# A pinned order for VectorE and ScalarE, a fourth load place and fewer warming products in the down stage of a decoder layer

## The chip, the cores and the metric

The kernel runs on one core of a Trainium2 chip. The metric is the device time of one execution in microseconds (us), as the median of several runs. TensorE (PE; its weight loads PEld) multiplies, VectorE (DVE), ScalarE (ACT) and GpSimd (POOL) work on tiles, and SyncE (SP) issues most transfers.

## The reference

One layer of a hybrid decoder, in float32, with 256 tokens and a model width of 2048:

```
h = RMSNorm(x);  z = h @ W_in
y = concat(PoolMixer(z_pool), MLA(z_q, z_kv, z_kr), MemXAttn(z_mq, mem)) @ W_o
x = x + y
h = RMSNorm(x)
x = x + (silu(conv(h @ W_gate)) * (h @ W_up)) @ W_down
```

The feed-forward width is 5632, and `conv` is causal over three tokens. The change lies in the last product, `a @ W_down`, where `a` is 256 x 5632 and `W_down` is 5632 x 2048, and in the first microseconds of the kernel.

## The kernel before, in words

**Splitting.** Every float32 weight is cut into a high part and a remainder. `split_w` (L88) does this for up to 1024 columns: ScalarE casts the weight to `wh` (L94), and VectorE subtracts `wh` from the weight to give `wl` (L95). Each of the two has three places. TensorE then makes three products of 512 columns for each sum: high by high, remainder of the activation by high, and high by remainder. In the down stage these are L740, L741 and L742, the three lines of `prod`. L742 alone reads `wl`.

**Loads.** `load_w` (L82) brings 1 MB of weights, 2048 columns, to one of three places of the tag `wr`. SP issues these loads in order (L85), and each waits until the place it needs is free.

**Stages.** First the memory's keys and values, before whose first product 16 products of ones keep TensorE at work (L159, L160) while the first loads arrive; then the input projection, the attention heads and the output projection; then `gemm_t` (L108, L111) for gate and up, 44 times, with `glu` after each; and from about 791 us the down stage.

**The down stage** (L735 to L823) makes two passes `c`, one for each half of the output's columns. A pass goes over 22 pairs `j` of feature blocks. A pair's weights are four blocks of 128 x 512, and its result is 2 token tiles by 2 column tiles.

- `plain` (L744) makes the 8 sums in the usual way, from two splits of 1024 columns. Thirteen pairs of a pass go this way: `j` = 0, 1, 3, 5, ..., 19, 20, 21. The last goes bank by bank.
- `seven` (L755) makes them from 7 sums of combined blocks, for `j` = 2, 4, ..., 18. VectorE forms the weights' differences: L760 two blocks at once (1024 columns), L763 and L764 one each. Splits follow: b11 (512 columns), b2, t13 and t24 (1024 each). t13 and t24 read the differences, which lie in `dn`; the trace calls their remainders `wl<-dn` and the others `wl<-wr`. Three of the seven sums go to the result's own banks, four to common ones (`com`).
- `common` (L775) fetches x1 for the output through POOL's queue (step 0), adds up the common sums (step 1), and adds these, scaled, to x1 (step 2).
- `finish` (L795) adds the own sums and writes the output. For the first pass it is called behind the first `plain` of the second.

`dn` is one tile of 16 blocks of 512 columns: blocks 0 to 7 hold the differences of two `seven`s in turn, 8 to 11 the common sums, 12 to 15 the output. It takes the place of the activation `h2`, which the gate and up products read.

**What sets the order.** The kernel is written in a framework that builds each engine's queue from its own estimate of when operands are ready. A queue is therefore not in the order of the source unless something forces it. Semaphores are set from the data that each instruction reads and writes. On the chip each queue runs in the order so built.

Of the kernel before, what the change touches and what calls it, by code (L numbers as in the profile page):

```python
# [11 lines left out]
F32 = mybir.dt.float32  # L12
# [3 lines left out]
ALU = mybir.AluOpType  # L16
AX = mybir.AxisListType

P = 128
# [17 lines left out]
STG = 2048  # L37
HS = 1024
NN = 512

PAIRS = KF // 2
SEVEN = tuple(range(2, 20, 2))
# [18 lines left out]
def layer(ctx, tc, xT_d, xn_d, memT_d, vec_d, tab_d, w_z_d, w_mqkr_d, w_q_d, w_kv_d, w_mem_d, w_pool_d, w_o_d,  # L61
          w_g_d, w_u_d, w_dn_d, out_d):
    nc = tc.nc

    const = ctx.enter_context(tc.tile_pool(name="const", bufs=1))
    stage = ctx.enter_context(tc.tile_pool(name="stage", bufs=1))
# [5 lines left out]
    def nm(s):  # L72
        uid[0] += 1
        return f"{s}_{uid[0]}"
# [7 lines left out]
    def load_w(src, n, cut=STG):  # L82
        raw = stage.tile([P, STG], F32, tag="wr", name=nm("wr"), bufs=3)
        for c in range(0, n, cut):
            nc.sync.dma_start(raw[:, c:min(n, c + cut)], src[:, c:min(n, c + cut)])  # L85
        return raw

    def split_w(raw, o, n, cut=HS):  # L88

        hi = stage.tile([P, HS], F32R, tag="wh", name=nm("wh"), bufs=3)  # L90
        lo = stage.tile([P, HS], F32R, tag="wl", name=nm("wl"), bufs=3)
        for c in range(0, n, cut):
            e = min(n, c + cut)
            nc.scalar.copy(hi[:, c:e], raw[:, o + c:o + e])  # L94
            nc.vector.tensor_tensor(lo[:, c:e], raw[:, o + c:o + e], hi[:, c:e].bitcast(F32), op=ALU.subtract)  # L95
        return hi, lo

    def gemm_t(ps, raw, o, act, ks, first=True, last=True):
# [57 lines left out]
    warm = const.tile([P, 1], F32, name="warm")  # L156
    nc.scalar.copy(warm[:], eps[:])
    ps = ps_aux()
    for _ in range(16):  # L159
        nc.tensor.matmul(ps[:, 0:P], ones[:], ones[:], start=True, stop=True)  # L160

    def rsqrt_(dst, src, scale):
# [73 lines left out]
    raw0 = stage.tile([P, STG], F32, tag="wr", name=nm("wr"), bufs=3)  # L236
# [181 lines left out]
    for m in range(6):  # L418
        raw = load_w(w_z_d[m], STG)
# [18 lines left out]
    for i in range(2):  # L438
        o = slice(2 * i, 2 * i + 2)
# [293 lines left out]


    dn = big.tile([P, 16, NN], F32, tag="act", name="dn")  # L735
    cnt = [0]

    def prod(ps, a, b, first, last):

# [4 lines left out]
    def plain(c, j, own, first, last, by_bank=False):  # L744
        raw = load_w(w_dn_d[c, j], STG)
        ws = [split_w(raw, k * HS, HS) for k in range(2)]
        order = [(k, t, n) for k in range(2) for t in range(NT) for n in range(2)]
        if by_bank:
            order.sort(key=lambda o: o[1:])
        for k, t, n in order:  # L750
            a = [aT[j][:, k, o + t * P:o + (t + 1) * P] for o in (0, T)]
            s = n if k == 0 else 1 - n
            prod(own[t, n], a, [w[:, s * NN:(s + 1) * NN] for w in ws[k]], first and k == 0, last and k == 1)

    def seven(c, j, own, com, first, last):  # L755
        raw = load_w(w_dn_d[c, j], STG)
        r3 = raw[:].rearrange("p (b n) -> p b n", n=NN)
# [7 lines left out]
        Ff = F.rearrange("p b n -> p (b n)")  # L765
        t13 = split_w(Ff, 0, HS)
        t24 = split_w(Ff, HS, HS)
        for (b, s), f, ps, own_ in (((b11, 0), 6, com[0], False), ((b2, 0), 5, own[0, 1], True),
                                    ((b2, 1), 0, own[0, 0], True), ((t13, 0), 2, com[1], False),
                                    ((t13, 1), 4, com[3], False), ((t24, 0), 3, com[2], False),  # L770
                                    ((t24, 1), 1, own[1, 0], True)):
            prod(ps, [aT[j][:, i, f, :] for i in range(2)], [w[:, s * NN:(s + 1) * NN] for w in b],
                 first and not own_, last and not own_)

    def common(c, com, step):  # L775

        v1, u2, u3, u5 = (dn[:, 8 + i, :] for i in range(4))
        if step == 0:
            for t in range(NT):
                for n in range(2):  # L780
                    o = c * HS + n * NN
                    nc.gpsimd.dma_start(dn[:, 12 + 2 * t + n, :], x1s[:, t, o:o + NN])
        elif step == 1:
            nc.scalar.copy(v1, com[0])
            nc.vector.tensor_tensor(u2, v1, com[2], op=ALU.add)
            nc.vector.tensor_tensor(u3, u2, com[3], op=ALU.add)
            nc.vector.tensor_tensor(u5, u3, com[1], op=ALU.add)
            nc.vector.tensor_tensor(u2, u2, com[1], op=ALU.add)
        else:
            for i, u in enumerate((v1, u2, u3, u5)):  # L790
                t = i // 2
                nc.vector.scalar_tensor_tensor(dn[:, 12 + i, :], u, rc[:, t:t + 1], dn[:, 12 + i, :],
                                               op0=ALU.mult, op1=ALU.add)

    def finish(c, own, eng):  # L795
        for t in range(NT):
            for n in range(2):
                o = dn[:, 12 + 2 * t + n, :]
                nc.vector.scalar_tensor_tensor(o, own[t, n], rc[:, t:t + 1], o, op0=ALU.mult, op1=ALU.add)
                eng.dma_start(out_d[t][:, c * HS + n * NN:c * HS + (n + 1) * NN], o)  # L800

    done = None
    for c in range(2):
        own_ps, com_ps = (ps_main, ps_aux) if c else (ps_aux, ps_main)
        own = {(t, n): own_ps()[:] for t in range(NT) for n in range(2)}
        com = None
        for j in range(PAIRS):
            if j in SEVEN:
                if com is None:
                    com = [com_ps()[:] for _ in range(4)]  # L810
                seven(c, j, own, com, j == SEVEN[0], j == SEVEN[-1])
# [12 lines left out]

# [83 lines left out]
```

## Time and profile before

| | before |
|---|---|
| median of 3 runs | 1030.2 us (1030.11 to 1031.09) |
| the profiled execution, its time | 1030.77 us |
| its span, first to last instruction | 1028.7 us |
| PE busy | 1018.4 us, 99% of the span |
| DVE busy | 760.3 us, 74% |
| ACT busy | 572.6 us, 56% |
| POOL busy | 15.3 us, 1% |
| transfers | 198.06 MB, mean 193 GB/s |
| TensorE's granted clock | 9 or more tenths in all 40 slices |

The span is what the trace covers; the execution's own time also holds what lies around it. A busy time counts an engine's work, not its waits. PE's ends are modelled and its products overlap, so an interval between two starts says more than the duration of one. In rows of a timeline a bracket holds the engine's idle time before the instruction and what ended it.

### The profile page before, as it was taken

The page shows a single profiled execution, that of the slowest core. Times are in us where ns is not written, and L with a number is a line of the kernel's source. Part 1 is how long each engine was busy: PE and PEld are TensorE (multiplying, and loading weights), DVE is VectorE, ACT ScalarE, POOL GpSimd, SP SyncE. Part 2 cuts the span into 40 slices and gives each one's busy share as a digit, 9 for nine tenths or more (in the row PEclk, how much of TensorE's full clock was granted, in tenths as well). Part 3 has the DMA queues.
Part 4 walks back from the last instruction along what each step waited for, and adds up shares of the span by engine and source line. Part 5 has one row for each costly group of instructions (what it writes and reads, how often), then busy time and mean ns, then how long its engine had stood idle before and what let it go on. Part 6 is the DMA issues. An engine that isn't in the chain of part 4 may idle for free.

```text
span 1028.7 us, 14089 instructions
## 1 busy us (share of the span) xinstructions
PE 1018.4 (99%) x5366; PEld 868.1 (84%) x5366; DVE 760.3 (74%) x1140; ACT 572.6 (56%) x850; POOL 15.3 (1%) x33
## 2 busy tenths in 40 slices
PE   9999999999999999999999999999999999989998
PEld 7798888877888888888888888888888888877886
DVE  7967689756577776776767677676767788877886
ACT  7847576644566455555555555554555465544653
POOL 0000000000000000000000000000000000010000
PEclk9999999999999999999999999999999999999999
DMA  9575444333765555545545555555555555565552
GB/s 343 204 264 202 147 181 164 133 124 123 232 213 181 194 195 177 202 176 193 196 175 203 180 189 197 175 202 183 186 200 207 201 210 204 205 245 205 205 198 89
DMA packets 30611, 198.06 MB, mean 193 GB/s; under 512 B 3536, under 2 KB 4048, under 8 KB 8656
## 3 DMA queue, kind: packets, MB, share of 16 engines
q1 hardware_dynamic: 28368, 189.44, 52.0%
q0 software_dynamic: 1888, 7.34, 1.9%
q8 instruction: 42, 0.69, 0.3%
q10 hardware_dynamic: 288, 0.38, 0.1%
q14 instruction: 25, 0.20, 0.1%
HBM read 192.96 MB, written 4.19 MB: 192 GB/s over the span
## 4 chain that ended last, share of the span: by engine, by line
PE 95%; DMA 2%; DVE 2%; ACT 0%; issue 0%; SPq 0%; DVEq 0%
PE psm L108 35%; PE psm L111 18%; PE psm L127 6%; PE psm L125 6%; PE psm L126 6%; PE psm L742 3%; PE psa L742 3%; PE psm L740 3%; PE psm L741 3%; PE psa L741 3%; PE psa L740 3%; DMA wr<-in_w_dn 1%; DVE wl L95 1%; PE psa L223 1%; PE psa L392 1%; DMA wr<-in_w_mem 1%
## 5 line engine op out<-in xcount | busy, mean ns | idle before, releaser
L94 ACT CAST wh<-wr 128x1024 fp32r<-128x1024 f32 (+2 forms) x360 | 362.0, 1007 | 366.7 <-PE psm L108 177.5
L95 DVE TENSOR_TENSOR wl<-wr,wh 128x1024 fp32r<-128x1024 f32 (+2 forms) x360 | 417.8, 1169 | 193.9 <-ACT wh L94 191.5
L108 PE MATMUL psm<-h,wh 128*128 128x512 f32 x1408 | 353.1, 392 | 0.0
L108 PEld LDWEIGHTS psm<-h,wh 128*128 128x128 f32 x1408 | 253.2, 189 | 45.2
L111 PEld LDWEIGHTS psm<-h,wl 128*128 128x128 f32 x1408 | 192.1, 190 | 13.7
L111 PE MATMUL psm<-h,wl 128*128 128x256 f32 x1408 | 196.3, 282 | 0.0
L94 ACT CAST wh<-dn 128x1024 fp32r<-128x1024 f32 x36 | 36.2, 1053 | 30.1 <-PE psm L741 15.1
L95 DVE TENSOR_TENSOR wl<-dn,wh 128x1024 fp32r<-128x1024 f32 x36 | 42.4, 1219 | 9.0 <-ACT wh L94 9.0
L685 DVE SCALAR_TENSOR_TENSOR gc<-g,vec,gc 128x255 f32<-128x255 f32 x88 | 42.2, 480 | 1.5
L108 PE MATMUL psm<-xg,wh 128*128 128x512 f32 x160 | 43.0, 401 | 0.0
L742 PE MATMUL psm<-wl,aT 128*128 128x512 f32 x104 | 40.6, 391 | 0.0
L742 PE MATMUL psa<-wl,aT 128*128 128x512 f32 x104 | 40.6, 390 | 0.0
L740 PE MATMUL psm<-wh,aT 128*128 128x512 f32 x104 | 40.5, 390 | 0.0
L740 PE MATMUL psa<-wh,aT 128*128 128x512 f32 x104 | 40.5, 389 | 0.0
L741 PE MATMUL psm<-wh,aT 128*128 128x512 f32 x104 | 40.5, 389 | 0.0
L741 PE MATMUL psa<-wh,aT 128*128 128x512 f32 x104 | 40.5, 389 | 0.0
L125 PE MATMUL psm<-wh,cat 128*128 128x512 f32 x96 | 38.5, 401 | 0.0
L127 PE MATMUL psm<-wl,cat 128*128 128x512 f32 x96 | 37.8, 394 | 0.0
L126 PE MATMUL psm<-wh,cat 128*128 128x512 f32 x96 | 37.6, 392 | 0.0
L108 PEld LDWEIGHTS psm<-xg,wh 128*128 128x128 f32 x160 | 28.8, 189 | 4.9
L760 DVE TENSOR_TENSOR dn<-wr 128x1024 f32<-128x1024 f32 x18 | 22.0, 1223 | 12.9 <-DMA wr<-in_w_dn 12.4
L742 PE MATMUL psa<-wl,aS 128*128 128x512 f32 x63 | 24.4, 395 | 3.6 <-DVE wl L95 3.6
(227 smaller groups left out, 1365.3 us busy)
## 6 DMA issues: line engine op xcount, KB each, us to landing
wr<-in_w_g SPq DMA_DIRECT2D x44, 1024.0 KB, 4.8
wr<-in_w_u SPq DMA_DIRECT2D x44, 1024.0 KB, 4.8
wr<-in_w_dn SPq DMA_DIRECT2D x44, 1024.0 KB, 4.8
wr<-in_w_o SPq DMA_DIRECT2D x16, 1024.0 KB, 4.9
wr<-in_w_z SPq DMA_DIRECT2D x10, 1024.0 KB, 4.8
wr<-in_w_mqkr SPq DMA_DIRECT2D x8, 576.0 KB, 3.7
wr<-in_w_mem SPq DMA_DIRECT2D x4, 1024.0 KB, 7.0
wr<-in_w_mem SPq DMA_DIRECT2D x7, 512.0 KB, 9.0
```

The lines of the kernel that those rows point to most:

```text
L94: nc.scalar.copy(hi[:, c:e], raw[:, o + c:o + e])
L95: nc.vector.tensor_tensor(lo[:, c:e], raw[:, o + c:o + e], hi[:, c:e].bitcast(F32), op=ALU.subtract)
L108: nc.tensor.matmul(ps[:, :2 * T], hi[:, i * P:(i + 1) * P], act(k), start=first and c + i == 0, stop=False, skip_group_check=True)
L111: nc.tensor.matmul(ps[:, T:2 * T], lo[:, i * P:(i + 1) * P], act(k)[:, 0:T], start=False, stop=end and i == len(kc) - 1, skip_group_check= ...
L125: nc.tensor.matmul(ps, xh, hi[:, i, o], start=first and i == 0, stop=False)
L126: nc.tensor.matmul(ps, xl, hi[:, i, o], start=False, stop=False)
L127: nc.tensor.matmul(ps, xh, lo[:, i, o], start=False, stop=last and i == nk - 1)
L685: nc.vector.scalar_tensor_tensor(gc[:, d:T], g[:, 0:T - d], v(w, f), gc[:, d:T], op0=ALU.mult, op1=ALU.add)
L740: nc.tensor.matmul(ps, a[0], b[0], start=first, stop=False)
L741: nc.tensor.matmul(ps, a[1], b[0], start=False, stop=False)
L742: nc.tensor.matmul(ps, a[0], b[1], start=False, stop=last)
L760: nc.vector.tensor_tensor(F[:, 0:2], r3[:, 1:3], r3[:, 0:2], op=ALU.subtract)
```

## The change

A helper `keep` puts an instruction behind whatever the source wrote last for the same engine. It is used on all splits and differences of the down stage from `j` = 3 of the first pass on, and on the sums of `common` and `finish`. Steps 1 and 2 of `common` and the first pass's `finish` move between the two splits of a `plain` call (`between`): step 1 into `j` = 20, step 2 into `j` = 21, `finish` into `j` = 0 of the second pass. In `seven` the order is now L760's differences, b11, the two single differences, b2, t13, t24, and the differences have four blocks of `dn` instead of eight, whose halves swap roles from call to call. The four blocks that this frees, 4 to 7, are the place of every fourth load of the down stage. The warming products at the start are 13 instead of 16.

```diff
+    def keep(ins, on=True):
+        return tc.keep_in_program_order(ins) if on else ins
...
-            nc.scalar.copy(hi[:, c:e], raw[:, o + c:o + e])
-            nc.vector.tensor_tensor(lo[:, c:e], raw[:, o + c:o + e], hi[:, c:e].bitcast(F32), op=ALU.subtract)
+            keep(nc.scalar.copy(hi[:, c:e], raw[:, o + c:o + e]), kept)
+            keep(nc.vector.tensor_tensor(lo[:, c:e], raw[:, o + c:o + e], hi[:, c:e].bitcast(F32), op=ALU.subtract),
+                 kept)
...
-    for _ in range(16):
+    for _ in range(13):
         nc.tensor.matmul(ps[:, 0:P], ones[:], ones[:], start=True, stop=True)
...
+    def load_dn(c, j):
+        cnt[1] += 1
+        if cnt[1] % 4:
+            return load_w(w_dn_d[c, j], STG)
+        raw = dn[:, 4:8].rearrange("p b n -> p (b n)")
+        nc.sync.dma_start(raw, w_dn_d[c, j])
+        return raw
...
-        ws = [split_w(raw, k * HS, HS) for k in range(2)]
+        ws = [split_w(raw, 0, HS, kept=kept)]
+        if between is not None:
+            between()
+        ws.append(split_w(raw, HS, HS, kept=kept))
...
-        F = dn[:, 4 * (cnt[0] % 2):4 * (cnt[0] % 2) + 4, :]
-        nc.vector.tensor_tensor(F[:, 0:2], r3[:, 1:3], r3[:, 0:2], op=ALU.subtract)
-        b11 = split_w(raw, 0, NN)
-        b2 = split_w(raw, 2 * NN, HS)
-        nc.vector.tensor_tensor(F[:, 2], r3[:, 2], F[:, 0], op=ALU.subtract)
-        nc.vector.tensor_tensor(F[:, 3], r3[:, 3], F[:, 2], op=ALU.subtract)
-        t13 = split_w(Ff, 0, HS)
-        t24 = split_w(Ff, HS, HS)
+        i = cnt[0] % 2
+        F13, F24 = dn[:, 2 * i:2 * i + 2], dn[:, 2 - 2 * i:4 - 2 * i]
+        keep(nc.vector.tensor_tensor(F13, r3[:, 1:3], r3[:, 0:2], op=ALU.subtract), kept)
+        b11 = split_w(raw, 0, NN, kept=kept)
+        keep(nc.vector.tensor_tensor(F24[:, 0], r3[:, 2], F13[:, 0], op=ALU.subtract), kept)
+        keep(nc.vector.tensor_tensor(F24[:, 1], r3[:, 3], F24[:, 0], op=ALU.subtract), kept)
+        b2 = split_w(raw, 2 * NN, HS, kept=kept)
+        t13 = split_w(F13.rearrange("p b n -> p (b n)"), 0, HS, kept=kept)
+        t24 = split_w(F24.rearrange("p b n -> p (b n)"), 0, HS, kept=kept)
...
+            kept = c > 0 or j > SEVEN[0]
...
-                plain(c, j, own, j == 0, j == PAIRS - 1, by_bank=j == PAIRS - 1)
-            if j == 0 and done is not None:
-                finish(0, done, nc.gpsimd)
+                between = None
+                if j == 0 and done is not None:
+                    between = lambda o=done: finish(0, o, nc.gpsimd)
+                elif j >= PAIRS - 2:
+                    between = lambda s=j - PAIRS + 3: common(c, com, s)
+                plain(c, j, own, j == 0, j == PAIRS - 1, kept, between, j == PAIRS - 1)
...
-            if j == PAIRS - 3:
-                common(c, com, 1)
-            if j == PAIRS - 2:
-                common(c, com, 2)
```

## Rows read from the trace of the kernel before

**Rows 1.** All instructions of L742: duration ns min/median/max, first and last start us.

```profile
L742 PE MATMUL psa<-wl,aT x104: 389/389/497, 791.8 to 905.9; 128*128 128x512 f32 x104
L742 PE MATMUL psm<-wl,aT x104: 388/389/504, 906.6 to 1024.3; 128*128 128x512 f32 x104
```

**Rows 2.** Timeline of PE (start us, us, what), 28 undisturbed products, first and last.

```profile
899.81 0.39 PE L742 MATMUL psa<-wl,aT 128*128 128x512 f32 x1
...
905.93 0.39 PE L742 MATMUL psa<-wl,aT 128*128 128x512 f32 x1
```

**Rows 3.** PE's waits, 790 to 1029 us: total us, times, longest.

```profile
PE psa L742 <- DVE wl L95: 3.6, 2, 2.8
PE psm L742 <- DVE wl L95: 0.4, 1, 0.4
```

**Rows 4.** Timeline of PE at late products.

```profile
836.31 0.45 PE L742 MATMUL psm<-wl,aS 128*128 128x512 f32 x1
...
919.53 0.39 PE L740 MATMUL psa<-wh,aS 128*128 128x512 f32 x1
922.67 0.50 PE L742 MATMUL psa<-wl,aS 128*128 128x512 f32 x1 [2.76 <-DVE wl L95]
923.01 0.39 PE L741 MATMUL psa<-wh,aS 128*128 128x512 f32 x1
...
934.52 0.73 PE L742 MATMUL psa<-wl,aS 128*128 128x512 f32 x2 [0.86 <-DVE wl L95]
```

**Rows 5.** Timeline of DVE at the longest wait.

```profile
919.53 1.23 DVE L760 TENSOR_TENSOR dn<-wr 128x1024 f32<-128x1024 f32 x1 [2.94 <-DMA wr<-in_w_dn]
...
921.40 2.35 DVE L95 TENSOR_TENSOR wl<-dn,wh 128x1024 fp32r<-128x1024 f32 x2
```

**Rows 6.** Timeline of DVE, PEld and PE at one of six undisturbed calls.

```profile
855.16 2.36 DVE L95 TENSOR_TENSOR wl<-dn,wh 128x1024 fp32r<-128x1024 f32 x2 [1.50 <-ACT wh L94]
...
856.44 0.19 PEld L742 LDWEIGHTS psm<-wl,aS 128*128 128x128 f32 x1
...
856.60 0.39 PE L742 MATMUL psm<-wl,aS 128*128 128x512 f32 x1
```

**Rows 7.** Timeline of DVE, the first operations of one `seven`.

```profile
947.36 1.22 DVE L760 TENSOR_TENSOR dn<-wr 128x1024 f32<-128x1024 f32 x1
948.50 0.68 DVE L95 TENSOR_TENSOR wl<-wr,wh 128x512 fp32r<-128x512 f32 x1
949.10 0.68 DVE L763 TENSOR_TENSOR dn<-wr,dn 128x512 f32<-128x512 f32 x1
949.82 0.69 DVE L764 TENSOR_TENSOR dn<-wr,dn 128x512 f32<-128x512 f32 x1
950.42 1.22 DVE L95 TENSOR_TENSOR wl<-wr,wh 128x1024 fp32r<-128x1024 f32 x1
```

**Rows 8.** Timeline of DVE, the third sum of `finish` at the end of the first pass.

```profile
904.99 0.75 DVE L799 SCALAR_TENSOR_TENSOR dn<-psa,rc,dn 128x512 f32<-128x512 f32 x1 [0.61 <-PE psa L742]
```

**Rows 9.** The page's DMA issues (KB, median us to landing), and one load in the chain.

```profile
wr<-in_w_dn SPq DMA_DIRECT2D x44, 1024.0 KB, 4.8
...
911.57 7.94 DMA wr<-in_w_dn
```

**Rows 10.** Timeline of SP, the fourth load of the down stage and the one behind.

```profile
790.18 6.55 SPq L85 DMA_DIRECT2D wr<-in_w_dn  x2
```

**Rows 11.** L160 by stretches: us, PE busy (x) PEld busy (x), PEclk, DMA share, GB/s.

```profile
3.00:5.00 2.00, 2.00 (x11) 2.00 (x11) 1.00 0.87 277
...
6.76:7.50 0.74, 0.74 (x7) 0.74 (x6) 1.00 0.90 280
```

**Rows 12.** Timeline of PE and ACT at the start.

```profile
7.51 0.48 PE L125 MATMUL psm<-wh,mg 128*128 128x512 f32 x1
...
8.87 1.15 ACT L94 CAST wh<-wr 128x512 fp32r<-128x512 f32 x2 [1.65 <-DMA wr<-in_w_mem]
...
11.27 0.51 PE L126 MATMUL psm<-wh,mg 128*128 128x512 f32 x1 [0.29 <-DVE mg L136]
```

More of the change, by code (lines that the diff above doesn't have):

```diff
@@ L85, in load_w, with split_w @@
             nc.sync.dma_start(raw[:, c:min(n, c + cut)], src[:, c:min(n, c + cut)])
-        return raw
-    def split_w(raw, o, n, cut=HS):
+        return raw[:]
+    def keep(ins, on=True):
+        return tc.keep_in_program_order(ins) if on else ins
+    def split_w(raw, o, n, cut=HS, kept=False):
         hi = stage.tile([P, HS], F32R, tag="wh", name=nm("wh"), bufs=3)
@@ L235, in layer @@
     xg = mp.tile([P, KD, 2 * T], F32R, tag="cat", name="xg")
-    raw0 = stage.tile([P, STG], F32, tag="wr", name=nm("wr"), bufs=3)
+    raw0 = stage.tile([P, STG], F32, tag="wr", name=nm("wr"), bufs=3)[:]
     for a, b in ((0, 1), (1, 2), (2, 4)):
@@ L735, in layer @@
     dn = big.tile([P, 16, NN], F32, tag="act", name="dn")
-    cnt = [0]
+    cnt = [0, 0]
+    def load_dn(c, j):
[5 more added lines that the diff above has]
+        return raw
     def prod(ps, a, b, first, last):
@@ L742, in prod, with plain @@
         nc.tensor.matmul(ps, a[0], b[1], start=False, stop=last)
-    def plain(c, j, own, first, last, by_bank=False):
-        raw = load_w(w_dn_d[c, j], STG)
-        ws = [split_w(raw, k * HS, HS) for k in range(2)]
+    def plain(c, j, own, first, last, kept, between=None, by_bank=False):
+        raw = load_dn(c, j)
+        ws = [split_w(raw, 0, HS, kept=kept)]
+        if between is not None:
+            between()
+        ws.append(split_w(raw, HS, HS, kept=kept))
         order = [(k, t, n) for k in range(2) for t in range(NT) for n in range(2)]
@@ L753, in plain, with seven @@
             prod(own[t, n], a, [w[:, s * NN:(s + 1) * NN] for w in ws[k]], first and k == 0, last and k == 1)
-    def seven(c, j, own, com, first, last):
-        raw = load_w(w_dn_d[c, j], STG)
-        r3 = raw[:].rearrange("p (b n) -> p b n", n=NN)
-        F = dn[:, 4 * (cnt[0] % 2):4 * (cnt[0] % 2) + 4, :]
+    def seven(c, j, own, com, first, last, kept):
+        raw = load_dn(c, j)
+        r3 = raw.rearrange("p (b n) -> p b n", n=NN)
+        i = cnt[0] % 2
         cnt[0] += 1
-        nc.vector.tensor_tensor(F[:, 0:2], r3[:, 1:3], r3[:, 0:2], op=ALU.subtract)
-        b11 = split_w(raw, 0, NN)
-        b2 = split_w(raw, 2 * NN, HS)
-        nc.vector.tensor_tensor(F[:, 2], r3[:, 2], F[:, 0], op=ALU.subtract)
-        nc.vector.tensor_tensor(F[:, 3], r3[:, 3], F[:, 2], op=ALU.subtract)
-        Ff = F.rearrange("p b n -> p (b n)")
-        t13 = split_w(Ff, 0, HS)
-        t24 = split_w(Ff, HS, HS)
+        F13, F24 = dn[:, 2 * i:2 * i + 2], dn[:, 2 - 2 * i:4 - 2 * i]
[6 more added lines that the diff above has]
+        t24 = split_w(F24.rearrange("p b n -> p (b n)"), 0, HS, kept=kept)
         for (b, s), f, ps, own_ in (((b11, 0), 6, com[0], False), ((b2, 0), 5, own[0, 1], True),
@@ L783, in common @@
         elif step == 1:
[L784 to L788, printed above, removed]
+            keep(nc.scalar.copy(v1, com[0]))
+            for u, a, b in ((u2, v1, com[2]), (u3, u2, com[3]), (u5, u3, com[1]), (u2, u2, com[1])):
+                keep(nc.vector.tensor_tensor(u, a, b, op=ALU.add))
         else:
@@ L791, in common @@
                 t = i // 2
-                nc.vector.scalar_tensor_tensor(dn[:, 12 + i, :], u, rc[:, t:t + 1], dn[:, 12 + i, :],
-                                               op0=ALU.mult, op1=ALU.add)
+                keep(nc.vector.scalar_tensor_tensor(dn[:, 12 + i, :], u, rc[:, t:t + 1], dn[:, 12 + i, :],
+                                                    op0=ALU.mult, op1=ALU.add))
     def finish(c, own, eng):
@@ L798, in finish @@
                 o = dn[:, 12 + 2 * t + n, :]
-                nc.vector.scalar_tensor_tensor(o, own[t, n], rc[:, t:t + 1], o, op0=ALU.mult, op1=ALU.add)
+                keep(nc.vector.scalar_tensor_tensor(o, own[t, n], rc[:, t:t + 1], o, op0=ALU.mult, op1=ALU.add))
                 eng.dma_start(out_d[t][:, c * HS + n * NN:c * HS + (n + 1) * NN], o)
@@ L810, in layer @@
                     com = [com_ps()[:] for _ in range(4)]
-                seven(c, j, own, com, j == SEVEN[0], j == SEVEN[-1])
+                seven(c, j, own, com, j == SEVEN[0], j == SEVEN[-1], kept)
             else:
-                plain(c, j, own, j == 0, j == PAIRS - 1, by_bank=j == PAIRS - 1)
-            if j == 0 and done is not None:
-                finish(0, done, nc.gpsimd)
+                between = None
[4 more added lines that the diff above has]
+                plain(c, j, own, j == 0, j == PAIRS - 1, kept, between, j == PAIRS - 1)
             if j == PAIRS - 6:
                 common(c, None, 0)
-            if j == PAIRS - 3:
-                common(c, com, 1)
-            if j == PAIRS - 2:
-                common(c, com, 2)
         done = own
```

## The prediction

> **What bounds the kernel now.** I read four views, from the whole to the single product. The page comes first: TensorE is its busiest engine by far, so only time in which TensorE waits can be won. Next come all instructions of L742, the third line of `prod`. The down stage has 26 `plain` calls of 8 sums and 18 `seven` calls of 7, three products each: 1002 products. L742 first starts at 791.8 us and last at 1024.3 us [rows 1], so 999 steps took 232.5 us. An undisturbed step takes (905.93 - 899.81) / 27 = 0.2267 us [rows 2], and 999 of them 226.5 us. The stage thus holds 6.0 us that are not products following each other. That is all that a change of order can win there.
>
> Then I read who ended TensorE's waits in this stage: always VectorE's L95, the remainder `wl` of a split, 4.0 us in three waits [rows 3]. The product rows say what a wait costs. From 919.53 to 922.67 is 3.14 us, and the step after it, to 923.01, takes 0.34: together 3.03 more than two plain steps, of which 2.76 are shown as idle. So a wait costs its idle time, 0.16 beside it, and 0.11 in the step behind. By that rule the wait at 934.52 (0.86 idle) costs 1.13, and the third one (0.4 idle) 0.66. Sum: 4.8 us. Beyond these there are six places where a product is late by 0.04 to 0.17 us, about 0.5 us together; the one at 836.31 stands for them (0.45 us long where 0.39 is usual) [rows 4].
>
> Last I read VectorE around the longest wait. At 919.53 it begins L760, the differences of the **next** `seven`, after 2.94 us in which it only waited for that load to land. Behind it, at 921.40, come the two remainders of the **current** `seven`'s differences, for which TensorE stands [rows 5]. So the order on VectorE is the cause: an instruction that TensorE needs late stands ahead of one that it needs now, and the former waits for a load.
>
> **The change, part by part.**
>
> *The pinned order.* From `j` = 3 of the first pass on, VectorE and ScalarE follow the written order, in which a `seven`'s splits t13 and t24 and both splits of the following `plain` stand ahead of the next L760. What this does can be seen in the run before, for at six of the 18 `seven`s the queue happened to stand so. One of them is at 855.16: VectorE has been idle for 1.50 us and waits only for ScalarE's cast. The remainder's weight load then goes at 856.44 and its product at 856.60, on TensorE's plain step [rows 6]. At the other five VectorE's idle time is 1.50 or 1.51 us, and no product is late. The written order therefore costs TensorE nothing, with 0.16 us left, and that chain (TensorE frees a place, ScalarE casts, VectorE subtracts) starts from TensorE's own products, so it should repeat alike.
>
> Has VectorE the time? By the starts of one call [rows 7] the operations ahead of those splits take 1.14 + 0.60 + 0.72 + 0.60 + 1.14 us (the newly written order is the same), and t13 and t24 take 1.14 each, the pair's 2.36 less the last one's 1.22 [rows 6]: 6.5 us. A `plain` has two such, 2.3. That is 8.8 us against 45 steps of 0.2267 = 10.2 us of TensorE. VectorE keeps up, with 1.4 us to spare. ScalarE has five full casts and a half one in the same 10.2 us.
>
> The trace also shows what speaks against a fixed order: a VectorE instruction that waits holds all behind it, 2.94 us at 919.53 [rows 5]. The Trainium skill, "TensorE: Matmul & The Clock Gate", under "Architectural detail", says the same as a rule: the queues of ScalarE and VectorE are strictly first in, first out. By that rule taken alone every wait in the written order would reach TensorE, as in rival D below, and the sum would be a loss; the trace agrees with the rule, with that 2.94 us. By the six calls the waits that are left in the written order are hidden, and I go by these.
>
> So the three waits and the four small places that lie at a t13 remainder go: 4.8 + 0.2 us. The two other small places lie beside the sums of `common`, whose steps now stand between the two splits of a `plain`. There VectorE issues four more operations of about 0.7 us, 2.8 us, beside 2.3 us of splits, while TensorE has 24 steps, 5.4 us: covered, tightest in the last `plain`, which goes bank by bank and wants its second split after three products. I take these 0.3 us as won too. The bounds of this part: nothing beyond the three waits, 4.8 us; all that is not plain steps, 6.0 us. I take **5.3 us**, the places counted one by one, which lies between.
>
> *What is late next.* In the second pass the closing sums of the first one (`finish`, four operations) stand between the two splits of the first `plain`. Each waits for its bank, as the third does at 904.99, and takes 0.75 [rows 8]; the last bank is done with the pass, at 906.3 (905.9 and 0.39) [rows 1]. Then come 0.75 of the fourth sum and 1.2 of the second split's remainder: ready 2.0 us after the pass ends. TensorE wants it after 14 products, at 3.2. Covered by 1.2 us; without the cover it would cost up to 2.0 us, once. POOL's output transfers start behind these sums as before, and its loads of x1s behind them; those are wanted only at the end of the pass.
>
> *One place for the sums, a fourth for loads.* No instruction is added, and the splits of the differences stay the same four. The two halves of the four blocks swap roles from one `seven` to the next, so that F13 overwrites what t24 read before the `plain` in between: no wait. A load can now be issued when the load four before it has been split, not three. A load takes 4.8 us in the median, but 7.94 where POOL's transfers run beside it [rows 9]. In the written order L760's turn comes four remainders behind 855.16, at 859.7, and the first product of that `seven` is eleven steps before 856.60, at 854.1 [rows 6]: 5.6 us. For the load that landed at 919.5 the turn is then 906.2 + 48 x 0.2267 + 5.6 = 922.7. So order alone would nearly do, and the fourth place lets that load start about a call earlier. The load for `j` = 3 of the first pass, issued at 790.18 [rows 10], must now wait until the gate and up products have left the block that `dn` takes, just before the stage's first products: about 1 us later, and SP's queue holds the next ones behind it. TensorE wants that load's splits 24 + 24 + 21 steps, 15.6 us, into the stage, and it lands 4.8 us into it. I cost it at nothing; the cover is some 8 us, with 2.4 for the splits taken off, and if it were gone 1 us would show once.
>
> *13 warming products.* Sixteen are 32 rows, two each. Three fewer are six rows, and the last seven take 0.74 us. Earlier rows come every 0.2 us (11 in 2 us), the last ones every 0.11 [rows 11]: TensorE has risen from its lower to its higher level, 1.2 to 2.4 GHz, while working without a break. The first real product, at 7.51, could come about 0.7 us earlier. But at 11.27 TensorE waits for VectorE's L136, and that work follows ScalarE's cast at 8.87, which waited for a load [rows 12]. Nothing in this chain starts earlier, so what is won at 7.5 is waited for at 11.3. Bounds: 0.7 us won, or, if the level rose later, a few tenths lost, which the same wait takes up. I take 0.
>
> *Sum.* The profiled execution took 1030.77 us, with a span of 1028.7: 1030.77 - 5.3 = 1025.5. It stands 0.57 above the median of the runs, 1030.2, so as a median **1024.9 us**.
>
> **The rivals.** The bound for "faster" and "slower" is 0.2%, 2.1 us, about what a measurement of this kernel can tell from no change: below 1028.1, above 1032.3.
>
> *A. The waits go, the warming is absorbed (the forecast):* 1024.9, chance 0.70.
>
> *B. The warming's 0.7 us come through as well,* if the early loads no longer end last at 11.27: 1024.2, chance 0.10.
>
> *C. The waits at the start of the second pass stay,* because slow loads are the cause and not the order: 3.03 + 1.13 us remain, 1024.9 + 4.2 = 1029.1. For it: the longest wait follows a load slowed to 7.94 us. Against: the remainder for which TensorE stood needs no load of its own. Chance 0.08. That one of them stays, or a new one of this size comes, 1026 to 1028: 0.06.
>
> *D. Slower: in a strict queue the t13 remainder comes late in every `seven`.* The place is the chain of [rows 6]; the price, in each of the 17 pinned calls, is what the remainder is late beyond 0.16 us, and 0.11 in the step behind. It decides against the change when VectorE reaches this remainder 2.0 us later than in the six calls (1.50 idle, 0.16 spare, 0.33 late): 17 x 0.44 = 7.5 us lost, more than the 5.3 won and the 2.1 of the bound. At 2.5 us it is 17 x 0.95 = 16 us, and 1041. For it: every wait on VectorE now holds all behind it. Against: 1.50 us idle in all six, and 1.4 us spare in each 10.2. Chance 0.06.
>
> *That the fourth place does nothing,* order alone being enough, gives the time of A and is in it.
>
> **How the numbers follow.** Faster: A, B and C's milder form, 0.86, of which 0.01 lies short of the bound: 0.85. No change: that and C's full form, 0.09. Slower: D, 0.06. The range reaches down to the 6.0 us bound with B (1030.2 - 6.0 - 0.7 = 1023.5, and 0.1 for the scatter of a median) and up to C's milder form: 1023.4 to 1028.3.
>
> **What would show it.** Right: no wait of TensorE for L95 behind 800 us; every pair of t13 and t24 remainders ahead of the next L760, with VectorE idle about 1.5 us before it and that put down to ScalarE; L760 no longer ended by a load; the last L742 near 1019; the first real product near 6.8 us, with more idle time near 11. Wrong: TensorE waiting 0.1 to 0.5 us at each `seven`, VectorE waiting in `finish` with TensorE behind it, or loads issued later than now.

## The result, and the profile after

| | before | after |
|---|---|---|
| median | 1030.48 us (1028.44 to 1033.25, 6 runs) | 1024.48 us (1024.35 to 1025.02, 6 runs) |
| the profiled execution, its time | 1030.77 us | 1024.43 us |
| its span | 1028.7 us | 1022.4 us |
| first to last start of a product of the down stage | 791.34 to 1024.34: 233.0 us | 790.71 to 1018.02: 227.31 us |

The changed kernel is faster: ratio 0.9944, with a 95% interval of [0.9934, 0.9954]. The two spans differ by 6.3 us: 5.69 in the down stage and 0.63 before it.

The page of the changed kernel, its first lines and the chain that ended last:

```profile
span 1022.4 us, 14093 instructions
PE 1015.3 (99%) x5360; PEld 866.2 (85%) x5360; DVE 759.9 (74%) x1140; ACT 572.7 (56%) x850; POOL 15.3 (1%) x33
...
PE 98%; DMA 1%; ACT 0%; DVE 0%; SPq 0%; issue 0%
```

VectorE and ScalarE do the work they did, and the time came out of TensorE's span. In the chain VectorE's share is now 0% (2% before) and that of transfers 1% (2% before).

The code moved by a few lines: a split is now L98 (cast) and L99 (remainder), L742 is L756, L760 is L779, `finish` is L815, and the warming products are L165. All instructions of L756, columns as in [rows 1]:

```profile
L756 PE MATMUL psa<-wl,aT x104: 389/389/389, 791.2 to 904.2; 128*128 128x512 f32 x104
L756 PE MATMUL psm<-wl,aT x104: 388/389/389, 904.9 to 1018.0; 128*128 128x512 f32 x104
```

The longest product is as long as the median one, where [rows 1] had 497 and 504 ns: none was late. TensorE's waits in the whole execution say it again (us in total, times, longest):

```profile
PE psa L165 <- DVE eps L158: 1.1, 1, 1.1
PE psm L132 <- DVE wl L99: 0.9, 1, 0.9
PE psm L130 <- ACT mg L140: 0.7, 2, 0.5
PE psm L131 <- DVE mg L141: 0.2, 1, 0.2
```

All are in the first 50 us; the three waits of [rows 3] are gone. VectorE's timeline, at a call in the first pass and at the start of the second, answers to [rows 5, 6, 8]:

```profile
853.81 2.36 DVE L99 TENSOR_TENSOR wl<-dn,wh 128x1024 fp32r<-128x1024 f32 x2 [1.39 <-ACT wh L98]
856.09 2.35 DVE L99 TENSOR_TENSOR wl<-wr,wh 128x1024 fp32r<-128x1024 f32 x2
858.36 1.22 DVE L779 TENSOR_TENSOR dn<-wr 128x1024 f32<-128x1024 f32 x1
...
904.68 0.75 DVE L815 SCALAR_TENSOR_TENSOR dn<-psa,rc,dn 128x512 f32<-128x512 f32 x1 [0.61 <-PE psa L756]
905.35 1.22 DVE L99 TENSOR_TENSOR wl<-wr,wh 128x1024 fp32r<-128x1024 f32 x1
...
916.46 2.36 DVE L99 TENSOR_TENSOR wl<-dn,wh 128x1024 fp32r<-128x1024 f32 x2 [1.54 <-ACT wh L98]
918.74 2.35 DVE L99 TENSOR_TENSOR wl<-wr,wh 128x1024 fp32r<-128x1024 f32 x2
921.01 1.22 DVE L779 TENSOR_TENSOR dn<-wr 128x1024 f32<-128x1024 f32 x1
```

Each pair of t13 and t24 remainders (`wl<-dn`) has the `plain`'s pair behind it and only then the next differences (L779), which start without a wait. The loads there were hardly quicker. Transfers issued from 903 to 925 us (count, KB, median us to landing), to be read beside [rows 9]:

```profile
wr<-in_w_dn SPq DMA_DIRECT2D x3, 1024.0 KB, 7.0
dn<-x1s POOLq DMA_DIRECT2D x4, 256.0 KB, 7.3
dn<-in_w_dn SPq DMA_DIRECT2D x1, 1024.0 KB, 8.8
```

They take 7 to 9 us and nothing waits for them.

### The profile page after: what moved, and what is told of

Same layout as the page of the kernel before. It is cut to its first block, busy times and chain, and to the rows that moved or that the text cites. A ratio compares the mean times of both kernels' runs of the same rounds, so it can differ in the third digit from the quotient of the medians.

```text
span 1022.4 us, 14093 instructions
## 1 busy us (share of the span) xinstructions
PE 1015.3 (99%) x5360; PEld 866.2 (85%) x5360; DVE 759.9 (74%) x1140; ACT 572.7 (56%) x850; POOL 15.3 (1%) x33
## 4 chain that ended last, share of the span: by engine, by line
PE 98%; DMA 1%; ACT 0%; DVE 0%; SPq 0%; issue 0%
PE psm L113 35%; PE psm L116 18%; PE psm L132 6%; PE psm L130 6%; PE psm L131 6%; PE psa L756 4%; PE psm L756 4%; PE psa L755 4%; PE psm L755 4%; PE psm L754 4%; PE psa L754 4%; PE psa L228 1%; PE psa L397 1%; PE psa L392 1%; PE psa L597 1%; DMA wr<-in_w_mem 1%
## 5 line engine op out<-in xcount | busy, mean ns | idle before, releaser
L98 ACT CAST wh<-wr 128x1024 fp32r<-128x1024 f32 (+2 forms) x338 | 339.0, 1004 | 352.1 <-PE psm L113 177.4
L99 DVE TENSOR_TENSOR wl<-wr,wh 128x1024 fp32r<-128x1024 f32 (+2 forms) x338 | 392.8, 1166 | 183.4 <-ACT wh L98 181.1
L99 DVE TENSOR_TENSOR wl<-dn,wh 128x1024 fp32r<-128x1024 f32 x58 | 67.8, 1220 | 26.3 <-ACT wh L98 26.3
L98 ACT CAST wh<-dn 128x1024 fp32r<-128x1024 f32 x58 | 59.2, 1052 | 38.3 <-PE psm L755 21.7
L756 PE MATMUL psa<-wl,aT 128*128 128x512 f32 x104 | 40.5, 389 | 0.0
L756 PE MATMUL psm<-wl,aT 128*128 128x512 f32 x104 | 40.5, 389 | 0.0
L688 ACT ACTIVATE gc<-g,vec 128x256 f32<-128x256 f32 x44 | 26.3, 597 | 0.0
L130 PE MATMUL psm<-wh,mg 128*128 128x512 f32 x64 | 25.3, 398 | 0.8 <-ACT mg L140 0.7
```

The source lines that it names most:

```text
L98: keep(nc.scalar.copy(hi[:, c:e], raw[:, o + c:o + e]), kept)
L99: keep(nc.vector.tensor_tensor(lo[:, c:e], raw[:, o + c:o + e], hi[:, c:e].bitcast(F32), op=ALU.subtract), kept)
L130: nc.tensor.matmul(ps, xh, hi[:, i, o], start=first and i == 0, stop=False)
L688: nc.scalar.activation(gc[:], g[:], AF.Identity, bias=v("conv_b", f), scale=v("cw2", f))
```

## The experiments

Twelve runs, each beside the kernel before on the same chip. "The stage" is the time from the first to the last start of a product of the down stage: 233.0 us before, 227.3 after. Ratios are against the kernel before, with their 95% intervals. A `...` marks what is left out of a diff or of a list of rows.

### Which part of the change does it?

**four_blocks**: the kernel before with the four blocks for differences and nothing else. Three load places, nothing pinned, 16 warming products.

```diff
...
-        F = dn[:, 4 * (cnt[0] % 2):4 * (cnt[0] % 2) + 4, :]
+        i = cnt[0] % 2
+        F13, F24 = dn[:, 2 * i:2 * i + 2], dn[:, 2 - 2 * i:4 - 2 * i]
...
```

> The kernel before, with the sums of seven in four blocks of dn as in the change, and nothing else: three load places, no pinned order, 16 warming products. The four blocks alone make the next call's L760 wait for the t24 split that reads the block it overwrites, so it cannot stand ahead of it. Theory (the order of L760 and the remainders is the cause): the waits of TensorE in the down stage go, first to last product of prod 227.3 to 227.8 us where the kernel before has 233.0, and about 5.3 us less time than before, ratio 0.9945 to 0.9955. Rival (the late loads are the cause, and only a fourth place mends them): the waits at the start of the second pass stay, 3 to 4.2 us of them, ratio 0.998 to 1.000.

Measured: 1024.89 us (1024.85 to 1024.94), ratio 0.9953 [0.9940, 0.9965]; the stage 227.77 us. Nearly all of the gain comes from what the change's words call a place for sums. The data do the pinning: the two blocks that a call's first differences overwrite are those from which t24 of the call before was split, so they must come behind that split, in whatever order the framework would like them. All instructions of L747, the third product here:

```profile
L747 PE MATMUL psa<-wl,aT x104: 389/389/499, 791.2 to 904.5; 128*128 128x512 f32 x104
L747 PE MATMUL psm<-wl,aT x104: 388/389/500, 905.2 to 1018.5; 128*128 128x512 f32 x104
```

PE's timeline at the one late place of the first pass:

```profile
888.41 0.39 PE L746 MATMUL psa<-wh,aT 128*128 128x512 f32 x1
888.72 0.50 PE L747 MATMUL psa<-wl,aT 128*128 128x512 f32 x1
889.05 0.39 PE L745 MATMUL psa<-wh,aT 128*128 128x512 f32 x1
```

Two steps of 0.31 and 0.33 us where 0.23 is usual, beside the sums of `common`, and the same near 1002.7: 0.4 us together, about what separates this stage from that of the changed kernel.

**pin_eight**: the pinned order and `between`, but eight blocks, three load places and 16 warming products.

```diff
...
-        F13, F24 = dn[:, 2 * i:2 * i + 2], dn[:, 2 - 2 * i:4 - 2 * i]
+        F13, F24 = dn[:, 4 * i:4 * i + 2], dn[:, 4 * i + 2:4 * i + 4]
...
-        if cnt[1] % 4:
-            return load_w(w_dn_d[c, j], STG)
-        raw = dn[:, 4:8].rearrange("p b n -> p (b n)")
-        nc.sync.dma_start(raw, w_dn_d[c, j])
-        return raw
+        return load_w(w_dn_d[c, j], STG)
```

(against the changed kernel, as are the diffs of the kernels with a pinned order below)

> The pinned order of the change, with common and finish between the splits, but the sums in eight blocks as before, three load places and 16 warming products. Theory (order): same as four_blocks, 227.3 to 227.8 us from first to last product, ratio 0.9945 to 0.9955. Rival (loads): 3 to 4.2 us of waits stay at the start of the second pass, ratio 0.998 to 1.000. Rival D of the prediction (a strict queue makes t13 late in every call) is already out for the changed kernel; here it would show as 0.1 us and more at each call.

Measured: 1024.84 us (1024.34 to 1025.81), ratio 0.9953 [0.9940, 0.9965]; the stage 227.29 us, no late product. So the order alone, put there by the pin, does all of it, with three places for loads. VectorE at the start of its second pass, where [rows 5] had the longest wait:

```profile
916.88 2.36 DVE L99 TENSOR_TENSOR wl<-dn,wh 128x1024 fp32r<-128x1024 f32 x2 [1.54 <-ACT wh L98]
919.16 2.35 DVE L99 TENSOR_TENSOR wl<-wr,wh 128x1024 fp32r<-128x1024 f32 x2
921.43 1.22 DVE L775 TENSOR_TENSOR dn<-wr 128x1024 f32<-128x1024 f32 x1
```

**place_unpinned**: the kernel before with the four blocks and the fourth load place (`load_dn` as in the change), nothing pinned.

> The kernel before with the four blocks and the fourth load place, no pinned order, 16 warming products. Theory (order): the fourth place adds nothing to four_blocks, same time within 0.3 us, and no L760 is ended by a load. Rival (loads): this one alone has the whole gain, 0.9945 to 0.9955, and is 3 us or more faster than four_blocks.

Measured: 1025.06 us (1024.63 to 1026.06), ratio 0.9956 [0.9943, 0.9970]; the stage 227.77 us, to the hundredth that of four_blocks, with its late places. The fourth place adds nothing.

**no_between**: the changed kernel with `finish` and the steps of `common` back behind the whole `plain`, still pinned.

```diff
-                if j == 0 and done is not None:
-                    between = lambda o=done: finish(0, o, nc.gpsimd)
-                elif j >= PAIRS - 2:
-                    between = lambda s=j - PAIRS + 3: common(c, com, s)
...
+            if j == PAIRS - 3:
+                common(c, com, 1)
+            if j == PAIRS - 2:
+                common(c, com, 2)
```

> The changed kernel with the steps of common and the first pass's finish written behind the plain calls, as before, instead of between their splits; they are pinned there. In four_blocks, where they are not pinned, a product beside the sums of common is late in each pass, 0.4 us in all; in the changed kernel none is. Theory (VectorE's queue is ahead of TensorE there, so any fixed place is covered): 227.3 us from the first to the last product of prod, and the time of the changed kernel within 0.3 us. Rival (the place between the splits is what saves the 0.4 us): 0.3 us and more slower, with a late product beside the sums.

Measured: 1024.2 us (1024.11 to 1025.47), ratio 0.9950 [0.9933, 0.9966]; the stage 227.32 us. The move between the splits is worth nothing. The late places of four_blocks are absent here too, so the pin, not the place of those operations, takes away its 0.4 us.

### Is it the place of one instruction?

**differences_first**: pin_eight once more, with its strict queue, three places and eight blocks; but each call's first differences are pinned ahead of t13 and t24 of the call before, where the kernel before often had them.

```diff
...
         b2 = split_w(raw, 2 * NN, HS, kept=kept)
+        if j + 2 in SEVEN:
+            load_ahead(c, j + 1)
+            differ(c, j + 2, kept or c > 0 or j >= SEVEN[0])
...
```

> The pinned order of the change with 16 warming products, three load places and eight blocks of sums, but pinned the other way round: the next call's L760 stands ahead of t13 and t24 of the current one, in every call instead of in some. A strict queue on VectorE is then kept and only the place of one instruction differs from pin_eight. Theory (that place is the cause): with three places the next load lands about when the t13 remainder is due, so TensorE waits 0.1 to 0.5 us at most of the 16 calls and 3 to 5 us at the start of the second pass: 230 to 237 us from the first to the last product of prod, 1027 to 1034 us in all. Rival (any strict order will do, the estimate's mixed order was the fault): 227.3 us, as pin_eight.

Measured: 1030.57 us (1029.58 to 1033.03), ratio 1.0005 [0.9995, 1.0014]; the stage 232.77 us. The whole gain is gone. TensorE's waits in the stage:

```profile
PE psa L752 <- DVE wl L99: 2.0, 1, 2.0
PE psm L752 <- DVE wl L99: 1.5, 2, 1.1
```

Timeline of ScalarE and VectorE at the longest of these waits:

```profile
917.76 2.00 ACT L98 CAST wh<-dn 128x1024 fp32r<-128x1024 f32 x2 [1.71 <-PE psm L751]
...
919.99 1.23 DVE L768 TENSOR_TENSOR dn<-wr 128x1024 f32<-128x1024 f32 x1 [2.67 <-DMA wr<-in_w_dn]
921.13 2.35 DVE L99 TENSOR_TENSOR wl<-dn,wh 128x1024 fp32r<-128x1024 f32 x2
```

That is [rows 5] again: the differences waiting for a load, and behind them the remainders, whose casts ScalarE has done by 919.76. Between this kernel and pin_eight only that instruction stands elsewhere, so its place is the cause. TensorE stands long only three times, in two calls, and elsewhere loses at most 0.36 us in a call and nothing in most, where 0.1 to 0.5 us at most calls were expected. The differences wait for a load in 15 calls, but in most of them the load lands within the time that VectorE has to spare.

### How much of the strict queue's time is spare?

**extra_difference** and **two_extra_differences**: the changed kernel with one or two more operations of 1.14 us on VectorE behind b2 of each `seven`, ahead of t13. Nothing reads what they write. The diff is that of two; with one, its second line is missing.

```diff
         b2 = split_w(raw, 2 * NN, HS, kept=kept)
+        keep(nc.vector.tensor_tensor(dn[:, 8:10], r3[:, 1:3], r3[:, 0:2], op=ALU.subtract), kept)
+        keep(nc.vector.tensor_tensor(dn[:, 10:12], r3[:, 1:3], r3[:, 0:2], op=ALU.subtract), kept)
```

> The changed kernel with one more VectorE operation in each seven, ahead of t13: the differences of L760 once more into unused blocks (1.14 us, nothing reads them). It measures how much VectorE has to spare there. Theory (VectorE idles 1.4 us ahead of the t13 remainder, and 8.8 of 10.2 us a pair are used): all hidden, 0 to 0.5 us slower than changed_again. Rival D of the prediction (the t13 chain has no slack to give): 0.2 us and more lost at each of the 18 calls, 4 to 20 us slower.

> The changed kernel with two more VectorE operations of 1.14 us ahead of t13 in each seven, whose results nothing reads. Theory (VectorE has 1.4 us to spare in each 10.2 us and 1.4 us of idle time ahead of the t13 remainder): the second one no longer fits. 8.8 + 2.3 = 11.1 us of VectorE against 10.2 of TensorE makes VectorE the bound: 0.9 us at each of 18 calls, 16 us in all, 1038 to 1044 us, with TensorE waiting for L99. Rival (more is hidden than counted): under 5 us.

Measured: one costs nothing, 1024.64 us (1024.10 to 1025.28), ratio 0.9949 [0.9936, 0.9963], the stage 227.21. Two give 1034.51 us (1033.63 to 1035.43), ratio 1.0042 [1.0027, 1.0057], the stage 236.97: 9.7 us more, where 16 were expected. VectorE's timeline with one:

```profile
853.26 1.22 DVE L784 TENSOR_TENSOR dn<-wr 128x1024 f32<-128x1024 f32 x1
854.73 2.36 DVE L99 TENSOR_TENSOR wl<-dn,wh 128x1024 fp32r<-128x1024 f32 x2 [0.25 <-ACT wh L98]
```

and with two:

```profile
846.93 1.22 DVE L785 TENSOR_TENSOR dn<-wr 128x1024 f32<-128x1024 f32 x1
848.07 4.62 DVE L99 TENSOR_TENSOR wl<-dn,wh 128x1024 fp32r<-128x1024 f32 x4
...
857.95 1.22 DVE L785 TENSOR_TENSOR dn<-wr 128x1024 f32<-128x1024 f32 x1
```

TensorE's waits in the stage with two:

```profile
PE psa L756 <- DVE wl L99: 2.4, 6, 0.4
PE psm L756 <- DVE wl L99: 2.0, 5, 0.4
```

The idle 1.39 us of the changed kernel fall to 0.25 with one, and are used up with two: the remainders follow without a gap, and VectorE has become the bound, with a period of 11.02 us (846.93 to 857.95) against 45 x 0.2267 = 10.2 of TensorE. At 0.8 us a call 17 calls would lose 14 us; VectorE starts each pass ahead, and the first calls use that up: products are late in every call only from 849.7 us on in the first pass and from 958.4 in the second. So the spare is over one operation of 1.14 us and under two, as the 1.4 us of the prediction had it.

### The start

**warm_13**: the kernel before with 13 warming products. **changed_warm_16**: the changed kernel with 16.

```diff
-    for _ in range(16):
+    for _ in range(13):
```

> The kernel before with 13 warming products instead of 16, and nothing else. Theory (the warming is absorbed, and the 0.63 us by which the changed kernel is ahead at 11 us comes from its third load landing at 8.19 instead of 8.85 us, by chance): ratio 0.9995 to 1.0005, and the products at 11 us start earlier only where that load lands earlier. Rival (fewer warming products bring the start forward by themselves): 0.6 us less, ratio 0.9990 to 0.9996, with the third load landing near 8.2 in every run with 13 and near 8.85 in every run with 16.

> The changed kernel with 16 warming products instead of 13. Theory (what the warming wins at 7 us is waited for at 11 us, and the start goes by the third load's landing): the same time as changed_again within 0.3 us, and the start of the first gate product follows the landing as in the other runs, whatever the number of warming products. Rival (13 is worth 0.6 us): 0.6 us slower than changed_again.

**changed_again**: the changed kernel unaltered.

> The changed kernel once more, as the yardstick for the next three on the same chip: 1024.4 to 1025.0 us, 227.3 us from the first to the last product of prod, no wait of TensorE there. Where the third load lands at 8.2 us the first gate product starts near 297.4; at 8.85 near 298.1.

Measured: warm_13 1030.61 us (1028.9 to 1031.34), ratio 1.0007 [0.9998, 1.0016]; changed_warm_16 1024.47 (1024.18 to 1025.39), 0.9949 [0.9933, 0.9964]; changed_again 1024.52 (1024.47 to 1024.69), 0.9947 [0.9934, 0.9960]. Three warming products are worth nothing, on either kernel. The 0.63 us ahead of the stage is another thing. The timeline of ScalarE's cast that waits for the third load (8.87 in [rows 12]) and of the first gate product, in the changed kernel:

```profile
8.21 1.14 ACT L98 CAST wh<-wr 128x512 fp32r<-128x512 f32 x2 [0.99 <-DMA wr<-in_w_mem]
...
297.44 1.85 PE L113 MATMUL psm<-h,wh 128*128 128x512 f32 x7
```

in changed_warm_16:

```profile
8.08 1.14 ACT L98 CAST wh<-wr 128x512 fp32r<-128x512 f32 x2 [0.78 <-DMA wr<-in_w_mem]
...
297.39 1.85 PE L113 MATMUL psm<-h,wh 128*128 128x512 f32 x7
```

and in two_extra_differences, which has 13:

```profile
9.56 1.14 ACT L98 CAST wh<-wr 128x512 fp32r<-128x512 f32 x2 [2.58 <-DMA wr<-in_w_mem]
...
298.77 0.48 PE L113 MATMUL psm<-h,wh 128*128 128x512 f32 x1
```

From this cast to the first gate product are 289.2 to 289.3 us in each; in the kernel before, too (8.87 to 298.07: 289.2). The third load's landing sets when everything behind it happens, and the cast behind it starts from 8.08 to 8.87 us in the runs with 16 products and from 7.94 to 9.56 in those with 13.

### A further step: the wait at 43 us

The largest wait that is left for VectorE's remainders is 0.9 us at 43 us. VectorE stands before it, since the sums of squares of the memory and of x share one place (`ssacc`). Its timeline in the changed kernel:

```profile
41.75 0.69 DVE L202 TENSOR_TENSOR ssacc<-s 128x512 f32<-128x512 f32 x1 [1.80 <-PE psa L215]
42.36 1.22 DVE L99 TENSOR_TENSOR wl<-wr,wh 128x1024 fp32r<-128x1024 f32 x1
```

**own_accumulator** gives the memory's sums a place of the tag `tok`:

```diff
...
-    ms = SumSq()
+    ms = SumSq(tok()[:].rearrange("p (a t) -> p a t", t=T))
```

> The changed kernel, and the sums of squares of mem in a place of their own (one of the tok places) instead of the one that the sums of squares of x take next. In the changed kernel the first sum of x waits for TensorE's col_sums to have read the old one, and the remainder behind it on VectorE makes TensorE wait 1.04 us at 42.4, and 0.11 in the step behind. Theory (a queue held by a place, as in the down stage): that wait goes, 1.1 us less than changed_again, 1023.3 to 1023.8. Rival (the remainder would be late anyway, or the wait moves on): the same as changed_again within 0.3 us.

Measured: 1023.97 us (1023.73 to 1024.55), ratio 0.9942 [0.9929, 0.9955], the lowest median of all. It is 0.5 us under the changed kernel, half of what was expected, and their runs overlap. VectorE no longer waits there, but does the rest of its queue first (timeline of VectorE and TensorE):

```profile
38.66 2.86 DVE L141 SCALAR_TENSOR_TENSOR xg<-xT,vec,xg 128x256 fp32r<-128x256 f32 x7
41.44 0.68 DVE L207 TENSOR_TENSOR ssacc<-ssacc,s 128x512 f32<-128x512 f32 x1
42.04 1.22 DVE L99 TENSOR_TENSOR wl<-wr,wh 128x1024 fp32r<-128x1024 f32 x1
...
43.31 0.73 PE L132 MATMUL psm<-wl,mg 128*128 128x512 f32 x2 [0.36 <-DVE wl L99]
```

The remainder starts at 42.04 instead of 42.36, and TensorE waits 0.36 us instead of 0.87 (the expectations count the whole delay of the product, 0.53 and 1.04).

**own_accumulator_pinned** also pins the splits of the last quarter of the memory's values ahead of the eight parts of x.

```diff
...
-                hi, lo = split_w(raw, i * HS, HS, 512 if n + c == 0 else HS)
+                hi, lo = split_w(raw, i * HS, HS, 512 if n + c == 0 else HS, n == 1 and c == 3)
+                if n == 1 and c == 3:
+                    x_parts(8 + i * 4, 12 + i * 4)
...
```

> own_accumulator, and in the last quarter of the memory's values the splits of the weights pinned ahead of the parts of x (x_parts) on ScalarE and VectorE. In own_accumulator the wait at 42 us shrank from 1.04 us to 0.53 because seven parts of x and a sum of squares still stood ahead of the remainder. Theory (order again): the wait goes, 0.6 us less than own_accumulator, 1023.2 to 1023.6 us. Rival (the parts of x are then late for the input projection at 55 us): the wait moves there, and the time is that of own_accumulator or more.

Measured: 1026.6 us (1025.79 to 1026.84), ratio 0.9962 [0.9949, 0.9974]: 2 us worse than the changed kernel. TensorE's timeline shows new waits:

```profile
49.48 0.50 PE L132 MATMUL psm<-wl,mg 128*128 128x512 f32 x1 [0.38 <-DVE wl L99]
...
58.51 0.40 PE L130 MATMUL psm<-wh,xg 128*128 128x288 f32 x1 [0.62 <-ACT mv L330]
```

In the down stage the pin gained because VectorE had 1.4 us to spare behind the pinned work; here something else was late at once; that this was the work put off is what the expectation argues, and no run takes it apart.

## Why the prediction was right, and where its parts were off

**The place and the cause.** The forecast, 1024.9 us, was that the three waits go and that they come from the order on VectorE. That is shown: they are gone, and they return, with the time (1030.57), when the one instruction alone is put back (differences_first against pin_eight).

**The size.** 5.3 us were taken for the stage, and it gave 5.69. In the kernel before, the three waits and six late places hold 13 steps that are long by more than 0.03 us, and their excess over 0.2267 is 5.33 us together: the count was right. The rest, 0.36 us, lies in the steps that the prediction called plain. Their mean is 0.2275 us in the kernel before and 0.2271 in the changed one, and the 67 plain steps from 920 to 940, about the two longest waits, average 0.2290. A dozen steps or more behind such a wait are longer as well, by up to a hundredth of a microsecond each; the step that failed is the rule that a wait costs its idle time, 0.16 and 0.11, and no more. The upper bound, 6.0, was as near to the truth as the count, but no order reached its floor: the changed stage, too, takes 0.4 us more than 1001 steps of 0.2267.

Part of the agreement is luck. The 5.3 us were read from one execution, in which the granted clock stayed at 1.00 through the stage. Most executions of the kernel before probably lose about 1.5 us to a lower clock (the last section has the figures), and the prediction has no term for that. The profile of warm_13, the kernel before but for its start, shows such an execution: its long steps hold 5.65 us, of which 1.6 are clock and only 4.05 waits and late places. The changed kernel is rid of both, so the sum came out near the forecast.

**"The written order costs TensorE nothing."** Right: VectorE's idle time ahead of t13 is 1.39 to 1.54 us in all 18 calls (predicted: about 1.5) and is put down to ScalarE's cast. The two kernels with extra operations measured the spare that the prediction had added up. The Trainium skill ("TensorE: Matmul & The Clock Gate", "Architectural detail") says that VectorE's queue is strictly first in, first out. The trace of differences_first agrees: the remainders' casts are done by 919.76 us, the first about a microsecond earlier, and VectorE, idle for 2.67 us until 919.99, takes neither remainder before the waiting differences. Such a queue decides nothing by itself here; what counts is which instruction stands at the head.

**The sums of `common` and `finish`.** The first pass's closing sums cost nothing, as costed. The 0.3 us beside `common` was won, but not by the move between the splits (no_between has it without), only by the pin.

**One place for the sums.** "No instruction is added ... no wait" was true and missed the point. The four blocks make a dependency that by itself puts the differences behind t24's split; four_blocks has 5.2 of the stage's 5.7 us. The prediction gave the whole gain to the pin.

**The fourth place.** That it does nothing stood as a rival within the forecast, and it is so: place_unpinned equals four_blocks. The price taken for it, nothing, was right too: the load for `j` = 3 of the first pass went out 0.24 us behind the stage's first product (1.16 ahead of it before) and took 8.3 us, and nothing waited for it. "Perfetto Trace Analysis" of the Trainium skill, "Optimization Strategy", says that a repeating gap can mean too few buffers. The runs here decide against that reading: the gaps went with three places.

**13 warming products.** Taken as 0, and it is 0. The start did come out 0.63 us earlier in the profiled execution, yet by the third load, which landed earlier. The first real product came at 6.15 us, not near 6.8, and that made no difference: what is early there waits at the load. So rival B's figure appeared for a reason that is not B's.

**The other rivals.** C, slow loads as the cause: from 903 to 925 us the loads take 6.8 us in the median in pin_eight and 7.6 in four_blocks, which have no wait there, and 7.2 in differences_first, which has. D, the t13 remainder late in every call: it needs over 1.14 us more work on VectorE than the change has, and with two extra operations it came, at 9.7 us.

Open: the parts do not add up, since the pin and the four blocks force the same order, so no run can give either its own share of the 5.2 us.

## What to carry to other kernels

When a busy engine waits for a short operation of another, look at what stands ahead of that operation in its queue: an instruction that is wanted later and waits for a load should stand behind it, whether by a written order or by a shared buffer whose dependency forces it. Where a change bundles several parts, try each alone, since two may do the same thing and a third nothing. And before making a queue strict, measure its slack by putting dummy operations into it: one free and two dear told here how much there was.

## What the runs showed of the hardware that was not expected

**A wait can cost TensorE its clock, or not.** In the profile of warm_13 TensorE waited 2.14 us at the same place as in [rows 4], and its granted clock then fell. TensorE's timeline:

```profile
921.23 0.50 PE L742 MATMUL psa<-wl,aS 128*128 128x512 f32 x1 [2.14 <-DVE wl L95]
...
922.49 0.63 PE L742 MATMUL psa<-wl,aS 128*128 128x512 f32 x1
922.92 0.63 PE L740 MATMUL psm<-wh,aS 128*128 128x512 f32 x1
```

Three stretches of the same trace (window: us, then PE, PEld, DVE, ACT, POOL busy and instructions, granted clock, DMA share, GB/s):

```profile
918.00:921.20 3.20, 1.09 (x5) 0.56 (x3) 3.08 (x4) 1.24 (x2) 0.00 (x0) 1.00 0.79 328
921.20:925.90 4.70, 4.67 (x13) 3.64 (x14) 4.61 (x5) 1.67 (x2) 0.00 (x0) 0.64 0.07 12
925.90:930.00 4.10, 4.10 (x19) 3.38 (x18) 1.26 (x2) 1.05 (x1) 0.00 (x0) 1.00 0.65 242
```

Eight products stepped by 0.43 us instead of 0.23 (the lower level, 1.2 instead of 2.4 GHz): 1.6 us on top of the wait. The kernel before had waited longer there, 2.76 us, and the granted clock stayed at 1.00 in its rows from 919 to 927. What makes the difference between the two was not found.

The mean granted clock of each execution tells how often the clock is lower. Of 47 executions of the kernel before, run beside the experiments, 33 have a mean of 0.998 or less, with a median of 1030.4 us, and 14 have 0.999 or 1.000, with a median of 1028.9. The 1.5 us between them are about what the eight slow products cost. In warm_13 the difference is smaller (1030.8 in 5 executions, 1030.3 in 6). None of the 50 executions of the kernels without these waits is under 0.999. So the lower clock goes with the waits, and it is a part of the scatter of the kernels that have them (1027.9 to 1033.3, against 1024.1 to 1026.1 in the changed kernel, four_blocks, pin_eight, place_unpinned and no_between). That in each of those executions it was one of these waits that took the clock is argued, not shown.

**TensorE's rise at the start varies.** From 3 to 5 us the warming products made 11 rows in the kernel before, 15 in the changed one, 11 in changed_again and 14 in four_blocks, which has 16 products. A row takes 0.2 us at the lower level and 0.11 at the higher [rows 11], so TensorE rose within these 2 us in two of the four runs and later in the others, whatever the count of products. (The profile's granted clock reads 1.00 in that window in all four, so the level is read from the spacing of the rows.) The Trainium skill ("TensorE: Matmul & The Clock Gate", "What's actually happening") says that the moment varies from run to run; these runs agree. In none of them did it move the end, for the third load lands after it.
